# A state-space branch: decays in two half tiles of another pool, two chunks prepared ahead of the state, each chunk's norm at once

## The chip, the cores and the metric

The kernel runs on one core of one Trainium2 chip. The metric is device time in microseconds (us) of that core, from a run of the whole program. TensorE does the matrix products, VectorE, ScalarE and GpSimd (DVE, ACT and POOL in the rows) the elementwise work, and the queue of SyncE (SP) issues nearly all the DMAs.

## The reference

One layer of a recurrent decoder: 2048 prompt tokens and 32 sample tokens (8 sequences of 4) go through four branches in parallel (Mamba-2 SSD, S5, mLSTM, HGRN2), whose results are gated, added and projected out. The change is in the first branch. Its scan goes over chunks of 128 tokens, with 8 heads in 2 groups, and its result is gated and normalised per token:

```python
def step(h, inp):
    xc, ac, bc, cc = inp
    acum = jnp.cumsum(ac, axis=1)
    seg = acum[:, :, None] - acum[:, None, :]
    decay = jnp.exp(jnp.where(tri[None, :, :, None, None], seg, -jnp.inf))
    cb = jnp.einsum('btgn,bsgn->btsg', cc, bc)
    y = jnp.einsum('btsg,btsgr,bsgrp->btgrp', cb, decay, xc)
    y = y + jnp.einsum('btgn,bgrpn->btgrp', cc, h) * jnp.exp(acum)[..., None]
    to_end = jnp.exp(acum[:, -1:] - acum)
    h = h * jnp.exp(acum[:, -1])[..., None, None] + jnp.einsum('bsgn,bsgr,bsgrp->bgrpn', bc, to_end, xc)
    return h, y
...
h, ys = lax.scan(step, h0, (to_chunks(x, q), to_chunks(a, q), to_chunks(bm, q), to_chunks(cm, q)))
...
y = y + xs * p['ssd_D'].astype(F32).reshape(SSD_GROUPS, SSD_RPG, 1)
y = y.reshape(bsz, L, BRANCH_W) * jax.nn.silu(z.astype(F32))
y = rmsnorm(y, p['ssd_norm_w'])
```

## The kernel before

The prompt is worked on in four blocks of 512 tokens; block 0 carries the sample's 32 tokens too. Every dense product is done in three passes, with the weights and the inputs split into a high and a low part (`whi`, `wlo`, `xhi`, `xlo`): ScalarE makes `whi` (L122), VectorE and GpSimd make the two halves of `wlo` (L125, L127). The dense products that appear below are the merge gates `pg` (L284 to L286), the mLSTM's `pt_so` (L173 to L175) and S5's gate `pj_s5gs` (L147 to L149).

Each branch is a Python generator that gives way after a part of its work. Two strings, ORDER0 for block 0 and ORDER for the others, say which generator goes on next: `S` is the state-space mix `ssd_mix`, `M` the merge gates, `w` S5's set-up (block 0 alone), `q0` to `q3` S5's quarters, `m0` to `m3` the mLSTM's heads. A scheduler then sets the order on each engine from this program; on its engine an instruction never passes the one ahead of it, and a DMA waits in SP's queue until the buffer it writes is free. Tiles come from pools with a fixed number of buffers: `tm` has 4 of 1280 columns, of which the gate `zs` holds 2 for a whole block; `cm` has 13 of 544 columns; the PSUM pool of the small products has 5.

The mix of a block begins with sums of the decays, which are written to DRAM as rows (`arow`). Then, chunk by chunk, `ssd_core` loads the chunk's rows to all partitions as one tile `D` of 128x1024 in `tm` (L532), adds the mask on GpSimd (L535), and takes eight exponentials on ScalarE (L537). TensorE makes C B (`pc`, L542) and the transposed x (`px`, L548). ScalarE copies `px` to `xs`; VectorE makes `xdt` (L553), then `xde`, which needs the last column of every head's `D` (L557), then multiplies `D` by `pc` (L560, two halves). `yi` (L564) is eight products of `D` with `xdt`. The state follows: `yo` from the state `ssd_h` (L625) and the chunk's own part `st` from `xde` (L626); VectorE updates `ssd_h` (L629, L630). `ssd_y` puts y together, gates it with `zs` on GpSimd (L577) and takes its squares on ScalarE (L578). After the last chunk the norm of all chunks is one chain of 13 short instructions on VectorE (L636, L637 and `rsqrt`, L97 to L102), ScalarE scales `zs` (L641), and TensorE transposes it (`ypt`, L647). The mLSTM's rows `mlr` and `mlq` come right behind.

## Time and profile before

| | |
|---|---|
| time of three runs | 3214.97 us median (3210.85 to 3215.8) |
| profiled execution, first to last instruction | 3211.8 us, mean granted TensorE clock 0.968 |
| TensorE busy | 3054.7 us, 95% of the span |
| VectorE, GpSimd, ScalarE busy | 58%, 38%, 33% |
| DMA | 107 GB/s on average |

The profiled execution is one execution of the program; no time of its own is recorded beside its span, and the span lies within the three runs. TensorE is busy for nearly all of it, so a stretch in which it waits, or runs at the lower of its two clocks, shows directly in the time. The granted clock is given as a share of full speed (1.00 is 2.4 GHz, 0.50 is 1.2 GHz).

### The profile page before, as it was taken

The numbers are of one execution on the slowest core, as the hardware profiler recorded it, in microseconds if no ns is written. First come the engines' busy times: TensorE is split into PE (matmuls) and PEld (weight loads), VectorE is DVE, ScalarE is ACT, GpSimd is POOL, SyncE is SP. The second block draws the span as 40 slices with busy tenths as digits, with TensorE's granted clock in tenths as the row PEclk, the third lists the DMA queues.
The fourth block names the chain that finished last, engine by engine and source line by source line (L and its number), as shares of the span: only waits on it lengthen the run. The fifth ranks groups of instructions, "written<-read, shape, count | busy, mean of one in ns | idle before, by whom it ended". The sixth has DMA issues, their size and how long they took to land. (4 is left out here: it accounts for less than half of the span.)

```text
span 3211.8 us, 48779 instructions
## 1 busy us (share of the span) xinstructions
PE 3054.7 (95%) x18559; PEld 2652.6 (83%) x18559; DVE 1860.6 (58%) x3808; ACT 1067.7 (33%) x2200; POOL 1235.1 (38%) x1147
## 2 busy tenths in 40 slices
...
GB/s 163 96 96 189 125 90 96 88 65 95 120 99 199 151 50 92 117 84 87 79 111 179 144 86 86 117 87 79 79 105 156 156 129 71 92 80 74 100 93 86
DMA packets 204958, 344.68 MB, mean 107 GB/s; under 512 B 87908, under 2 KB 124676, under 8 KB 204724
## 3 DMA queue, kind: packets, MB, share of 16 engines
...
## 5 line engine op out<-in xcount | busy, mean ns | idle before, releaser
L127 POOL TENSOR_TENSOR wlo<-wraw,whi 128x384 fp32r<-128x384 f32 (+1 forms) x412 | 615.4, 1494 | 1196.7 <-ACT whi L122 1141.0
L125 DVE TENSOR_TENSOR wlo<-wraw,whi 128x640 fp32r<-128x640 f32 (+2 forms) x416 | 430.6, 1036 | 649.7 <-ACT whi L122 624.7
L122 ACT CAST whi<-wraw 128x1024 fp32r<-128x1024 f32 (+1 forms) x416 | 435.9, 1048 | 860.3 <-issue 319.3
L286 PE MATMUL pg<-xhi,wlo 128*128 128x512 f32 (+1 forms) x1280 | 463.1, 362 | 0.0
L284 PE MATMUL pg<-xhi,whi 128*128 128x512 f32 (+1 forms) x1280 | 461.9, 361 | 0.1
L285 PE MATMUL pg<-xlo,whi 128*128 128x512 f32 (+1 forms) x1280 | 458.9, 359 | 0.0
L286 PEld LDWEIGHTS pg<-xhi,wlo 128*128 128x128 f32 x1280 | 245.8, 192 | 35.9 <-issue 4.0
L285 PEld LDWEIGHTS pg<-xlo,whi 128*128 128x128 f32 x1280 | 245.7, 192 | 32.2 <-issue 0.9
L284 PEld LDWEIGHTS pg<-xhi,whi 128*128 128x128 f32 x1280 | 245.8, 192 | 31.2 <-issue 0.8
L326 PE MATMUL pb<-yh,whi 128*128 128x512 f32 (+1 forms) x640 | 227.2, 355 | 0.8 <-DVE acc L330 0.8
L328 PE MATMUL pb<-yh,wlo 128*128 128x512 f32 (+1 forms) x640 | 225.9, 353 | 0.0
L327 PE MATMUL pb<-yl,whi 128*128 128x512 f32 (+1 forms) x640 | 225.5, 352 | 0.0
L333 POOL TENSOR_TENSOR acc<-acc,gth 128x512 f32<-128x512 f32 (+1 forms) x120 | 138.4, 1154 | 192.3 <-DVE gth L332 169.3
L173 PE MATMUL po<-whi,mhi 128*128 128x256 f32 (+1 forms) x544 | 155.6, 286 | 8.1 <-ACT po L369 8.1
L174 PE MATMUL po<-wlo,mhi 128*128 128x256 f32 (+1 forms) x544 | 154.8, 284 | 0.0
L175 PE MATMUL po<-whi,mlo 128*128 128x256 f32 (+1 forms) x544 | 154.6, 284 | 0.0
L326 PEld LDWEIGHTS pb<-yh,whi 128*128 128x128 f32 x640 | 120.4, 188 | 18.2 <-issue 1.3
L327 PEld LDWEIGHTS pb<-yl,whi 128*128 128x128 f32 x640 | 120.4, 188 | 16.9 <-issue 0.6
L328 PEld LDWEIGHTS pb<-yh,wlo 128*128 128x128 f32 x640 | 120.3, 188 | 16.1
L332 DVE SCALAR_TENSOR_TENSOR gth<-gth,pb 128x512 f32<-128x512 f32 (+1 forms) x120 | 70.1, 584 | 94.3 <-PE pb L328 90.9
L877 POOL TENSOR_TENSOR hk<-hk,hC 128x256 f32<-128x256 f32 (+1 forms) x96 | 72.9, 759 | 110.9 <-PE hpa L854 53.1
L173 PEld LDWEIGHTS po<-whi,mhi 128*128 128x128 f32 (+1 forms) x544 | 102.0, 188 | 9.3 <-ACT po L369 8.8
...
## 6 DMA issues: line engine op xcount, KB each, us to landing
...
```

Of the source, the lines that this page charges most:

```text
L122: nc.scalar.copy(hi, raw)
L125: nc.vector.tensor_tensor(lo[:, :d], raw[:, :d], hi[:, :d].bitcast(F), op=OP.subtract)
L127: nc.gpsimd.tensor_tensor(lo[:, d:], raw[:, d:], hi[:, d:].bitcast(F), op=OP.subtract)
L173: nc.tensor.matmul(ps, xh, hi[:, k % 4], start=(k == 0), stop=False)
L174: nc.tensor.matmul(ps, xh, lo[:, k % 4], start=False, stop=False)
L175: nc.tensor.matmul(ps, xl, hi[:, k % 4], start=False, stop=(k == KT - 1))
L284: nc.tensor.matmul(pg, gh[:, k], self.xhi[k][:, o:o + n], start=(k == 0), stop=False)
L285: nc.tensor.matmul(pg, gh[:, k], self.xlo[k][:, o:o + n], start=False, stop=False)
L286: nc.tensor.matmul(pg, gl[:, k], self.xhi[k][:, o:o + n], start=False, stop=(k == KT - 1))
L326: nc.tensor.matmul(pb, bh[:, k], yh[k][:, o:o + n], start=(k == 0), stop=False)
L327: nc.tensor.matmul(pb, bh[:, k], yl[k][:, o:o + n], start=False, stop=False)
L328: nc.tensor.matmul(pb, bl[:, k], yh[k][:, o:o + n], start=False, stop=(k == 3))
```

## The change

- **D.** A chunk's decays are two tiles of 128x512 (`D_0`, `D_1`: a group of four heads each) in pool `cm`, each with its own DMA, its own mask on GpSimd and its own four exponentials.
- **xdt and xde.** Both are products with `px` straight from PSUM on VectorE. The factor of `xde` is a new small tile `dte` = exp(total - sum) * dt/8, made once in a block. ScalarE's copy `xs` serves the skip term alone. `xdt` and `xde` take turns in two role tiles each.
- **Order of the chunks.** `ssd_core` prepares a chunk; the new `ssd_chunk` does `yi`, `yo`, `st`, y and the state. They go 0, 1, then state 0, 2, state 1, 3, state 2, state 3, and the generator gives way after each.
- **Norm.** `ssd_y` ends with the chunk's own norm (13 short instructions for one column) and scaling.
- **Order strings.** In ORDER0 the S5 set-up `w` and the merge gates `M` stand elsewhere among the parts of `S`; in ORDER `S*2 M S*7` stands for `S M S*4`.

The rest of the file differs only in comments.

```diff
     def ssd_core(self, nb, c, m):
         nc = self.nc
         samp = m == NS
         o = c * P
         neg = self.negs if samp else self.neg
         nm = f"{nb}_{c}"
-        D = self.tm.tile([P, 1280], F, tag="tm", name=f"D{nm}", bufs=TMB)[:m, :8 * m]
-        self.dq.dma_start(D, self.arow[c // 4][8 * (c % 4):8 * (c % 4) + 8]
-                          .rearrange("h t -> (h t)").partition_broadcast(m))
-        D = D.rearrange("p (h t) -> p h t", h=8)
-        nc.gpsimd.tensor_tensor(D, D, neg.unsqueeze(1).to_broadcast([m, 8, m]), op=OP.add)
-        for h in range(8):
-            nc.scalar.activation(D[:, h], D[:, h], AF.Exp, bias=self.nac[:m, c, h:h + 1])
+        D = [self.cm.tile([P, TX], F, tag="cm", name=f"D{nm}_{g}", bufs=CMB)[:m, :4 * m] for g in range(2)]
+        for g in range(2):
+            r = 8 * (c % 4) + 4 * g
+            self.dq.dma_start(D[g], self.arow[c // 4][r:r + 4].rearrange("h t -> (h t)").partition_broadcast(m))
+            D[g] = D[g].rearrange("p (h t) -> p h t", h=4)
+            nc.gpsimd.tensor_tensor(D[g], D[g], neg.unsqueeze(1).to_broadcast([m, 4, m]), op=OP.add)
+            for h in range(4):
+                nc.scalar.activation(D[g][:, h], D[g][:, h], AF.Exp, bias=self.nac[:m, c, 4 * g + h:4 * g + h + 1])
         pc = self.psum(None, f"pc{nm}").rearrange("p (r t) -> p r t", r=4)[:m]
         BT, CT = self.xbc[4][:, o:o + m], [t[:, o:o + m] for t in self.CTm]
         for g in range(2):
@@ -547,22 +548,41 @@
         for j in range(4):
             nc.tensor.transpose(px[:, j * P:(j + 1) * P], self.xbc[j][:, o:o + m], self.ident)
         hv = lambda t: t.rearrange("p (h d) -> p h d", h=8)
+        mul = lambda e, out, v: e.tensor_tensor(hv(out), hv(px), v.unsqueeze(2).to_broadcast([m, 8, 64]), op=OP.mult)
+        xdt = self.role("be"[c % 2], f"xdt{nm}")[:m, :512]
+        mul(nc.vector, xdt, self.dtq[:m, c])
+        for g in range(2):
+            nc.vector.tensor_tensor(D[g], D[g], pc[:, g:g + 1, :m].to_broadcast([m, 4, m]), op=OP.mult)
+        xde = self.role("cf"[c % 2], f"xde{nm}")[:m, :512]
+        mul(nc.vector, xde, self.dte[:m, c])
         xs = self.role("a", f"xs{nm}")[:m, :512]
         nc.scalar.copy(xs, px)
-        xdt = self.role("b", f"xdt{nm}")[:m, :512]
-        nc.vector.tensor_tensor(hv(xdt), hv(xs), self.dtq[:m, c].unsqueeze(2).to_broadcast([m, 8, 64]), op=OP.mult)
         nc.gpsimd.tensor_tensor(hv(xs), hv(xs), self.Dh[:m].unsqueeze(2).to_broadcast([m, 8, 64]), op=OP.mult)
-        xde = self.role("c", f"xde{nm}")[:m, :512]
-        te = self.te_s if samp else D[:, :, 127]
-        nc.vector.tensor_tensor(hv(xde), hv(xdt), te.unsqueeze(2).to_broadcast([m, 8, 64]), op=OP.mult)
-        for g in range(2):
-            Dg = D[:, 4 * g:4 * g + 4]
-            nc.vector.tensor_tensor(Dg, Dg, pc[:, g:g + 1, :m].to_broadcast([m, 4, m]), op=OP.mult)
-        yi = self.psum(None, f"yi{nm}")[:m]
+        return D, xdt, xs, xde, Bt, CT
+    def ssd_intra(self, nb, c, m, D, xdt):
+        nc = self.nc
+        yi = self.psum(None, f"yi{nb}_{c}")[:m]
         for h in range(8):
             hs = slice(h * 64, (h + 1) * 64)
-            nc.tensor.matmul(yi[:, hs], D[:, h], xdt[:, hs], start=True, stop=True)
-        return yi, xs, xde, Bt, CT
+            nc.tensor.matmul(yi[:, hs], D[h // 4][:, h % 4], xdt[:, hs], start=True, stop=True)
+        return yi
+    def ssd_chunk(self, nb, c, dec, D, xdt, xs, xde, Bt, CT):
+        nc = self.nc
+        yo = self.psum(None, f"yo{nb}_{c}")
+        st = self.psum(None, f"st{nb}_{c}")
+        yi = self.ssd_intra(nb, c, P, D, xdt)
+        for g in range(2):
+            gs = slice(g * 64, (g + 1) * 64)
+            cs = slice(g * 256, (g + 1) * 256)
+            nc.tensor.matmul(yo[:, cs], CT[g], self.ssd_h, start=True, stop=True)
+            nc.tensor.matmul(st[gs, 0:256], Bt[:, gs], xde[:, cs], start=True, stop=True)
+        self.ssd_y(nb, c, P, yi, yo, xs)
+        hv = self.ssd_h.rearrange("p (r d) -> p r d", r=4)
+        nc.vector.tensor_tensor(hv, hv, dec[:, c].unsqueeze(2).to_broadcast([P, 4, 64]), op=OP.mult)
+        nc.vector.tensor_tensor(self.ssd_h, self.ssd_h, st[:, 0:256], op=OP.add)
...
             nc.scalar.activation(xs[:, qs], self.zs[q][:m, c], AF.Square, accum_out=self.yss[:m, q, c:c + 1])
 
+        v = self.sp.tile([P, 5], F, tag="yv", name=f"yv{nm}", bufs=2)
+        nc.vector.tensor_tensor(v[:m, 0:1], self.yss[:m, 0, c:c + 1], self.yss[:m, 1, c:c + 1], op=OP.add)
+        nc.vector.tensor_scalar(v[:m, 0:1], v[:m, 0:1], 1.0 / 512, 4 * EPS, op0=OP.mult, op1=OP.add)
+        rs = self.rsqrt(v[:, 0:1], "yr", m)
+        for q in range(2):
+            nc.scalar.mul(self.zs[q][:m, c], self.zs[q][:m, c], rs)
...
+        self.dte = self.sp.tile([P, 5, 8], F, tag="dte", name=f"dte{nb}", bufs=1)
+        nc.vector.tensor_tensor(fl(self.dte[:, 0:4]), fl(self.nac[:, 0:4]), pe[:, 32:64], op=OP.add)
+        nc.scalar.activation(fl(self.dte[:, 0:4]), fl(self.dte[:, 0:4]), AF.Exp)
+        nc.vector.tensor_tensor(self.dte[:, 0:4], self.dte[:, 0:4], self.dtq[:, 0:4], op=OP.mult)
...
         self.yss = self.sp.tile([P, 2, 5], F, tag="yss", name=f"yss{nb}", bufs=1)
-        if nb == 0:
-            nc.vector.memset(self.yss, 1.0)
         yield
-        for c in range(4):
-            yi, xs, xde, Bt, CT = self.ssd_core(nb, c, P)
-            yo = self.psum(None, f"yo{nb}_{c}")
-            st = self.psum(None, f"st{nb}_{c}")
-            for g in range(2):
-                gs = slice(g * 64, (g + 1) * 64)
-                cs = slice(g * 256, (g + 1) * 256)
-                nc.tensor.matmul(yo[:, cs], CT[g], self.ssd_h, start=True, stop=True)
-                nc.tensor.matmul(st[gs, 0:256], Bt[:, gs], xde[:, cs], start=True, stop=True)
-            self.ssd_y(nb, c, P, yi, yo, xs)
-            hv = self.ssd_h.rearrange("p (r d) -> p r d", r=4)
-            nc.vector.tensor_tensor(hv, hv, dec[:, c].unsqueeze(2).to_broadcast([P, 4, 64]), op=OP.mult)
-            nc.vector.tensor_tensor(self.ssd_h, self.ssd_h, st[:, 0:256], op=OP.add)
+        core = {}
+        for c in (0, 1, -1, 2, -2, 3, -3, -4):
+            if c >= 0:
+                core[c] = self.ssd_core(nb, c, P)
+            else:
+                self.ssd_chunk(nb, -1 - c, dec, *core.pop(-1 - c))
             yield
         if nb == 0:
             self.ssd_sample(nb)
-        v = self.sp.tile([P, 5], F, tag="yv", name=f"yv{nb}", bufs=1)
-        nc.vector.tensor_tensor(v[:, :ncc], self.yss[:, 0, :ncc], self.yss[:, 1, :ncc], op=OP.add)
-        nc.vector.tensor_scalar(v[:, :ncc], v[:, :ncc], 1.0 / 512, 4 * EPS, op0=OP.mult, op1=OP.add)
-        rs = self.rsqrt(v[:, :ncc], "yr")
-        for (c, o, m) in self.chunks(nb):
-            for q in range(2):
-                nc.scalar.mul(self.zs[q][:m, c], self.zs[q][:m, c], rs[:m, c:c + 1])
...
-        self.te_s = self.sp.tile([NS, 8], F, tag="te_s", name="te_s", bufs=1)
-        nc.scalar.activation(self.te_s, pe[:NS, 8:16], AF.Exp)
+        nc.scalar.activation(self.dte[:NS, 4], pe[:NS, 8:16], AF.Exp)
+        nc.vector.tensor_tensor(self.dte[:NS, 4], self.dte[:NS, 4], self.dtq[:NS, 4], op=OP.mult)
...
-        yi, xs, xde, Bt, CT = self.ssd_core(nb, 4, NS)
+        D, xdt, xs, xde, Bt, CT = self.ssd_core(nb, 4, NS)
+        yi = self.ssd_intra(nb, 4, NS, D, xdt)
...
-ORDER0 = ("z*2 i x*3 z w u x*3 u*2 S u S*3 w S*2 w*7 q2*2 q0 M q0*2 M*2 q1 M*5 q1 g0*8 q1 q2 q3 o q3*2 o*6 r "
+ORDER0 = ('z*2 i x*3 z w u x*3 u*2 w S u S*4 M S M S w S*5 M w*6 q2*2 q0 M q0*2 q1 M*4 q1 g0*8 q1 q2 q3 o q3*2 o*6 r
-ORDER = ("u x u z q0*2 x u q0 z q1*2 M z u x*3 q2*2 x q1 M*2 q3*3 M S M*2 q2 S M S*4 o r M m0 o m0 m1 m0*2 o "
+ORDER = ('u x u z q0*2 x u q0 z q1*2 M z u x*3 q2*2 x q1 M*2 q3*3 M S M*2 q2 S*2 M S*7 o r M m0 o m0 m1 m0*2 o
```

On TensorE, block 1, behind the state of chunk 0: before, the products `pc_1` and `px_1` that prepare chunk 1 come only here.

```order
L625 MATMUL yo_0_11894<-ssd_h,CT_0_11471 128x256
L626 MATMUL st_0_11895<-xde_0_11881,Bt_0_11869 64x256
L625 MATMUL yo_0_11894<-ssd_h,CT_1_11472 128x256
L626 MATMUL st_0_11895<-xde_0_11881,Bt_0_11869 64x256
L542 MATMUL pc_1_11955<-CT_0_11471,cv_xbc_1_11427 128x128
L542 MATMUL pc_1_11955<-CT_1_11472,cv_xbc_1_11427 128x128
L543 MATMUL pc_1_11955<-cst,cv_xbc_1_11427 128x128
L548 MATMUL px_1_11961<-cst,cv_xbc_1_10728 128x128
L548 MATMUL px_1_11961<-cst,cv_xbc_1_10971 128x128
L548 MATMUL px_1_11961<-cst,cv_xbc_1_11339 128x128
L548 MATMUL px_1_11961<-cst,cv_xbc_1_11383 128x128
```

After the change `pc_1` (and, 14 rows of S5 later, `px_1`) stands ahead of the first `yi`:

```order
L549 MATMUL px_0_11960<-cst,cv_xbc_1_11465 128x128
L543 MATMUL pc_1_11988<-CT_0_11553,cv_xbc_1_11509 128x128
L543 MATMUL pc_1_11988<-CT_1_11554,cv_xbc_1_11509 128x128
L544 MATMUL pc_1_11988<-cst,cv_xbc_1_11509 128x128
L284 MATMUL pg_0_6_0_12016<-xhi_0_10324,whi_12011 128x512
L285 MATMUL pg_0_6_0_12016<-xlo_0_10325,whi_12011 128x512
L286 MATMUL pg_0_6_0_12016<-xhi_0_10324,wlo_12013 128x512
L284 MATMUL pg_0_6_0_12016<-xhi_1_10331,whi_12011 128x512
```

and behind the state of chunk 0 stand only five products of S5's gate and the preparation of chunk 2, then `yi_1`:

```order
L543 MATMUL pc_2_12099<-CT_1_11554,cv_xbc_1_11509 128x128
L544 MATMUL pc_2_12099<-cst,cv_xbc_1_11509 128x128
L147 MATMUL pj_s5gs_1_0_12332<-xhi_0_10324,whi_12327 128x512
L148 MATMUL pj_s5gs_1_0_12332<-xlo_0_10325,whi_12327 128x512
L149 MATMUL pj_s5gs_1_0_12332<-xhi_0_10324,wlo_12329 128x512
L147 MATMUL pj_s5gs_1_0_12332<-xhi_1_10331,whi_12327 128x512
L148 MATMUL pj_s5gs_1_0_12332<-xlo_1_10332,whi_12327 128x512
L549 MATMUL px_2_12105<-cst,cv_xbc_1_10810 128x128
L549 MATMUL px_2_12105<-cst,cv_xbc_1_11053 128x128
L549 MATMUL px_2_12105<-cst,cv_xbc_1_11421 128x128
L549 MATMUL px_2_12105<-cst,cv_xbc_1_11465 128x128
L568 MATMUL yi_1_12121<-xdt_1_11999,D_1_0_11974 128x64 x4
```

So chunk 1's preparation moved ahead of chunk 0's state. Before, 20 rows of `pg` stood between `px_1` and `yi_1`; behind `yo_3`, after the change, stand 22 rows of `pg` with the transposes `ypt` and `mlr` among them, until the last `ypt` of chunk 3.

On SP's queue, block 1, with the semaphores that each DMA waits for (PE, DVE, Pool and Activation are engines, DMAHW other transfers), before:

```order
L1619 DMA s5c_2_11820<-dLC_1004 128x1024 [waits DMAHW5_49,PE_49]
L120 DMA wraw_12419<-in_win_dram 128x1024 [waits DMAHW3_49,DVE_49,Pool_49]
L532 DMA D_0_11854<-arow_11737 128x1024 [waits DMAHW4_49,DMAHW7_49,DMAHW0_49,PE_49]
L532 DMA D_1_11944<-arow_11737 128x1024 [waits DMAHW2_49,PE_49]
L1637 DMA s5gd_2_10655<-s5g_2_11822 128x8x64 [waits DMAHW6_49,DVE_49]
L1653 DMA s5gr_0_12172<-s5gd_0_10653 128x512
L1653 DMA s5gr_1_12413<-s5gd_1_10654 128x512 [waits Activation_49]
L120 DMA wraw_12459<-in_win_dram 128x1024 [waits DMAHW1_49,DVE_49,Pool_49]
L532 DMA D_2_12000<-arow_11737 128x1024 [waits DMAHW4_49,DVE_49,PE_49]
L120 DMA wraw_12506<-in_win_dram 128x1024 [waits DMAHW3_49,DVE_49,Pool_49]
L532 DMA D_3_12056<-arow_11737 128x1024 [waits DMAHW5_49,DVE_49,PE_49]
```

and after:

```order
L1637 DMA s5c_2_11906<-dLC_1004 128x1024 [waits DMAHW2_49,PE_49]
L534 DMA D_0_0_11940<-arow_11819 128x512 [waits DMAHW5_49,DMAHW0_49]
L534 DMA D_0_1_11941<-arow_11819 128x512 [waits DMAHW1_49]
L534 DMA D_1_0_11974<-arow_11819 128x512
L534 DMA D_1_1_11975<-arow_11819 128x512 [waits DMAHW3_49]
L534 DMA D_2_0_12085<-arow_11819 128x512 [waits DMAHW4_49]
L534 DMA D_2_1_12086<-arow_11819 128x512
L1671 DMA s5gr_0_12318<-s5gd_0_10735 128x512 [waits DMAHW6_49]
L1671 DMA s5gr_1_12559<-s5gd_1_10736 128x512 [waits DMAHW7_49,DVE_49]
L1655 DMA s5gd_2_10737<-s5g_2_11908 128x8x64 [waits DMAHW0_49,DVE_49]
L120 DMA wraw_12565<-in_win_dram 128x1024 [waits DMAHW1_49,Pool_49]
L534 DMA D_3_0_12162<-arow_11819 128x512 [waits DMAHW2_49,PE_49]
```

The loads of chunks 0 to 2 now stand in one piece behind `s5c_2` and wait for no engine; those of chunk 3 wait for TensorE, with a weight load ahead of them and another behind.

On VectorE, block 1, after the change: the short instructions of a chunk's norm (`yv_0`, `yr_t`, `yr_y`, 128x1) stand between the products that prepare chunk 3 and those of y and the state (`y`, `ssd_h`).

```order
L585 TENSOR_TENSOR ssd_h<-ssd_h,st_1_12120 128x256
L101 SCALAR_TENSOR_TENSOR yr_t<-yr_t,yv_0_12065 128x1
L551 TENSOR_TENSOR xdt_3_12187<-px_3_12182,dtq_11813 128x512
L102 SCALAR_TENSOR_TENSOR yr_y<-yr_t,yr_y 128x1
L555 TENSOR_TENSOR D_3_0_12162<-D_3_0_12162,pc_3_12176 128x512
L100 TENSOR_TENSOR yr_t<-yr_y 128x1
L555 TENSOR_TENSOR D_3_1_12163<-D_3_1_12163,pc_3_12176 128x512
L101 SCALAR_TENSOR_TENSOR yr_t<-yr_t,yv_0_12065 128x1
L601 TENSOR_TENSOR yv_1_12142<-yss_11835 128x1
L551 TENSOR_TENSOR xde_3_12191<-px_3_12182,dte_11828 128x512
L102 SCALAR_TENSOR_TENSOR yr_y<-yr_t,yr_y 128x1
L602 TENSOR_SCALAR yv_1_12142<-yv_1_12142 128x1
```

Before, the norm's instructions stood in one row behind all four chunks.

## Rows read from the trace of the kernel before

**Rows 1.** The page, busy time of each engine.
```profile
PE 3054.7 (95%) x18559; PEld 2652.6 (83%) x18559; DVE 1860.6 (58%) x3808; ACT 1067.7 (33%) x2200; POOL 1235.1 (38%) x1147
```

**Rows 2.** Windows of blocks 1 and 0: length, busy, TensorE clock, DMA share, GB/s.
```profile
1107.00:1191.00 84.00, 72.24 (x370) 57.74 (x370) 43.08 (x60) 32.86 (x87) 37.71 (x29) 0.84 0.24 79
...
117.00:266.00 149.00, 116.53 (x701) 98.44 (x700) 106.73 (x177) 57.16 (x182) 88.83 (x92) 0.80 0.40 104
```

**Rows 3.** TensorE's waits in block 1, 1107 to 1206: total, times, longest.
```profile
PE yi L564 <- ACT D L537: 6.0, 2, 3.5
PE yi L564 <- DVE D L560: 3.0, 1, 3.0
PE mlq L1042 <- ACT mlQ L1032: 2.1, 1, 2.1
PE ypt L647 <- ACT zs L641: 2.0, 1, 2.0
```

**Rows 4.** TensorE's waits in block 0, 117 to 266.
```profile
PE yi L564 <- ACT acc L287: 9.3, 1, 9.3
PE yi L564 <- issue: 6.7, 2, 3.8
PE ypt L647 <- ACT zs L641: 4.5, 1, 4.5
PE sts L713 <- DVE y L572: 3.8, 1, 3.8
```

**Rows 5.** Windows at either clock, columns as in rows 2.
```profile
217.00:223.80 6.80, 5.96 (x26) 5.78 (x26) 0.48 (x3) 4.79 (x11) 0.00 (x0) 0.50 0.66 97
...
1142.00:1152.20 10.20, 10.20 (x35) 7.65 (x35) 2.28 (x5) 1.76 (x6) 1.89 (x3) 0.50 0.30 103
...
1173.10:1177.30 4.20, 4.20 (x25) 2.98 (x25) 0.98 (x2) 0.66 (x2) 0.00 (x0) 1.00 0.00 0
...
1141.80:1149.40 7.60, 7.57 (x25) 5.14 (x25) 1.43 (x3) 1.24 (x5) 0.23 (x1) 0.51 0.41 138
```

**Rows 6.** Timelines around the first yi of block 1: start, length, [idle before].
```profile
1113.35 0.80 SPq L532 DMA_DIRECT2D D<-arow  x2
...
1119.74 2.46 ACT L537 ACTIVATE D<-D,nac 128x128 f32<-128x128 f32 x8 [1.27 <-POOL D L535]
...
1122.29 1.86 DVE L557 TENSOR_TENSOR xde<-xdt,D 128x512 f32<-128x512 f32 x1 [1.89 <-ACT D L537]
...
1125.13 2.15 PE L564 MATMUL yi<-xdt,D 128*128 128x64 f32 x9 [2.48 <-ACT D L537]
```

**Rows 7.** Timelines of GpSimd and VectorE ahead of chunk 1's yi.
```profile
1134.96 2.85 POOL L535 TENSOR_TENSOR D<-D,neg 128x1024 f32<-128x1024 f32 x1
...
1135.47 3.26 DVE L1665 TENSOR_TENSOR s5gs<-s5gs,s5gr 128x512 f32<-128x512 f32 x1
...
1138.65 1.22 DVE L557 TENSOR_TENSOR xde<-xdt,D 128x512 f32<-128x512 f32 x1
...
1141.05 1.27 DVE L560 TENSOR_TENSOR D<-D,pc 128x512 f32<-128x512 f32 x2
```

**Rows 8.** Timelines of VectorE and GpSimd at block 1's norm.
```profile
1184.03 1.01 POOL L127 TENSOR_TENSOR wlo<-wraw,whi 128x384 fp32r<-128x384 f32 x1 [1.09 <-ACT whi L122]
...
1182.00 0.97 DVE L636 TENSOR_TENSOR yv<-yss 128x4 f32<-128x4 f32 x1
...
1184.21 0.86 DVE L100 TENSOR_TENSOR yr_t<-yr_y 128x4 f32<-128x4 f32 x1
...
1185.88 0.16 DVE L102 SCALAR_TENSOR_TENSOR yr_y<-yr_t,yr_y 128x4 f32<-128x4 f32 x1
```

**Rows 9.** Timeline of VectorE, first and last instruction of block 0's norm.
```profile
207.63 0.20 DVE L636 TENSOR_TENSOR yv<-yss 128x5 f32<-128x5 f32 x1 [1.02 <-ACT xs L578]
...
217.09 0.15 DVE L102 SCALAR_TENSOR_TENSOR yr_y<-yr_t,yr_y 128x5 f32<-128x5 f32 x1
```

**Rows 10.** A product on VectorE that reads PSUM, block 1: ns min/median/max.
```profile
L572 DVE TENSOR_TENSOR y<-yo,ea x4: 690/692/692, 1131.9 to 1176.8; 128x512 f32<-128x512 f32 x4
```

More of the change, by code (lines that the diff above doesn't have):

```diff
@@ L633, in ssd_mix @@
             self.ssd_sample(nb)
-        v = self.sp.tile([P, 5], F, tag="yv", name=f"yv{nb}", bufs=1)
-        nc.vector.tensor_tensor(v[:, :ncc], self.yss[:, 0, :ncc], self.yss[:, 1, :ncc], op=OP.add)
-        nc.vector.tensor_scalar(v[:, :ncc], v[:, :ncc], 1.0 / 512, 4 * EPS, op0=OP.mult, op1=OP.add)
-        rs = self.rsqrt(v[:, :ncc], "yr")
-        for (c, o, m) in self.chunks(nb):
-            for q in range(2):
-                nc.scalar.mul(self.zs[q][:m, c], self.zs[q][:m, c], rs[:m, c:c + 1])
+            yield
         for j in range(4):
```

7 lines of the change are left out of this document (2 added, 5 removed).

## The prediction

> **What bounds the kernel now.** I read the page first: TensorE is busy for 95% of the span [rows 1], so a gain has to come from the 5% in which it waits, or from stretches in which its clock is low. The windows of the stages with the state-space chunks show both: the 84 us of block 1 have 72.2 us of TensorE work at a mean granted clock of 0.84, the 149 us of block 0 have 116.5 at 0.80 [rows 2]. Third come the waits in those windows. In block 1 TensorE waits 6.0 + 3.0 us for `yi`, 2.0 for `ypt` and 2.1 for `mlq` [rows 3]; blocks 2 and 3 repeat these rows to within 0.6 us, which makes 39 us for three blocks. Block 0 has 9.3 + 6.7 us at `yi`, 4.5 at `ypt` and 3.8 at `sts`, 24 in all [rows 4].
>
> Behind most of these waits the clock is 0.50, its lower level of 1.2 GHz: 6.8 us behind block 0's `ypt`, 10.2 us behind the wait for chunk 1 in block 1 [rows 5]. There are five such stretches in block 0 (47.7 us) and eleven in blocks 1 to 3 (85 us, three of them behind `mlq`). What one costs is read from two runs of the same 25 chunk products: 7.6 us at the lower level, 4.2 behind chunk 3's wait of only 0.8 us, where the clock stayed at 1.00 [rows 5]. That is 45% of the slow time: 38 us in blocks 1 to 3, 21 in block 0.
>
> **Why `yi` waits.** For chunk 0 it is the decay tile. Its DMA is issued at 1113.35, when a `tm` buffer comes free; the exponentials run from 1119.74, `xde` from 1122.29 because it needs their last column, and `yi` starts at 1125.13 [rows 6]. For chunk 1 it is VectorE. `px_1` comes only behind the state of chunk 0, and then S5's `s5gs`, `xde`, a weight part and the product `D` follow one another until 1142.3, the `s5gs` for 3.26 us because GpSimd's mask runs from 1134.96 to 1137.81 [rows 7].
>
> **The change part by part, blocks 1 to 3.**
> *Half tiles in the other pool.* On SP's queue the six loads of chunks 0 to 2 stand behind `s5c_2` and wait for no engine. Chunk 0's load no longer waits until 1113.35 for a buffer; the masks and exponentials of two halves are the same work as one tile's. More instructions on SP (two issues of 0.4 us for one, [rows 6]) cost nothing while the weight loads behind them are early; if that cover is gone they cost 4 x 0.4 = 1.6 us a block.
> *xdt and xde from PSUM.* The nearest row is `y<-yo`, a product of the same size that reads PSUM: 0.69 us, four times within 2 ns [rows 10]. `xde` took 1.86 and 1.22 [rows 6, 7]. I take 0.69 for both products, which frees some 6 us of VectorE in a block; at worst they cost what they cost now, and nothing is freed. The new `dte` is three short VectorE instructions in a block, under 1 us, long before it is needed.
> *Two chunks ahead.* `px_k`, `xdt` and `D*pc` are done a whole chunk before `yi_k`; 4.2 us of TensorE's chunk work then cover some 2.7 us of VectorE (two products of 0.69, two that take 1.27 together, [rows 7]). So all 9 us of `yi` waits go, and their slow stretches.
> *Norm per chunk.* This is the term that gives something back. Before, 13 short instructions took from 1182.00 to 1186.04, so 0.31 us each: most take 0.16, but `yr_t` took 0.86, ending with GpSimd's weight part (1184.03 + 1.01), and `yv` 0.97 [rows 8]. Now there are 52 in a block, on an engine that does not let the next product pass. Behind the state of chunk 2 the norms of chunks 2 and 3 are both still to do: 26 x 0.31 = 8.1 us, with y and the state (four products of 0.4 to 0.7, some 2.2) and two `s5gs` (0.7 and up to 3.3, [rows 7]) some 14 us. TensorE's cover behind `yo_3` is 22 merge products of 512 columns, at 2.4 GHz 0.21 us each, and the small transposes, about 7 us together. So `ypt` of chunk 3 waits about 7 us where it waited 2.0. Such a wait drops the clock once: 3 us more by the slow stretch of 6.8 us [rows 5]. I add 2 for small waits in between. This is 12 us a block. Its lower bound is 4, if a short instruction takes 0.16; its upper 21, if it takes 0.52, as in block 0: 9.6 us for 13 with 2.8 us of others among them [rows 9].
> *mlq.* The 96 `pt_so` products now stand between `mlr` and `mlq`, so its 2.1 us and the slow stretch go.
>
> Together: 39 of waits and 38 of clock, 77 removed, less 3 x 12 given back, leaves 41.
>
> **Block 0.** 24 us of waits and 21 of clock, 45, are the upper bound. But VectorE is busy for 106.7 of 149 us there [rows 2], and S5's set-up, which now stands behind the chunks, is VectorE work. The 13 short instructions (6.8 us) become 65, 20 to 34 us at 0.31 to 0.52, and ten products save some 7. VectorE then has 113 to 127 us of work. It is now 72% busy, since it too waits for the chunks; with their waits gone I let it reach 90%, so the stage takes 125 to 141 us, 8 to 24 less. I take 15. At today's 72% it would be longer than now; I keep -10 as the lower bound.
>
> **Sum.** 41 + 15 = 56 us. The profiled execution's span of 3211.8 lies 3 us below the median, inside the runs; the difference is taken from the median: 3215 - 56 = 3159.
>
> **Two rules weighed.** On VectorE and GpSimd, [rows 8] show a VectorE instruction of 0.16 us that ends 0.03 us after GpSimd's, and [rows 7] one that ends behind the mask. The Trainium skill, "SBUF — State Buffer", section "SBUF: two separate sides", says that an instruction of VectorE with two SBUF inputs and one of GpSimd exclude each other for the whole instruction. These rows agree. By the row's mean of 0.31 us the sum stands; by the rule at its worst, every short instruction meeting a GpSimd one, the norm would cost what the slower rival below says. On the clock, [rows 5] show 1.00 behind a wait of 0.8 us and 0.50 behind waits of 3.5 and 4.5 us [rows 3, 4]. The Trainium skill's "TensorE: Matmul & The Clock Gate", section "A second HAM failure mode: psum-queue depth-cycling", says that short idle moments between groups of matmuls, as PSUM buffers go round, can keep the clock moving between its levels. Chunk 3's run in block 1 does not show that; by the rule the outcome is the clock rival below.
>
> **The rivals.**
> *Nothing given back.* The short instructions fall between GpSimd's, put-back 4 us a block, and block 0 gains 30: 65 + 30 = 95, 3120 us. For it: without `yv` and the one of 0.86, the other 11 of block 1 share 2.2 us [rows 8]. Against it: GpSimd's 37.7 us of work in the stage now fall into some 62 us instead of 84.
> *The waits move.* Short instructions at 0.52, put-back 21 us, and block 0 gains nothing because S5's set-up is late: 14 us, 3201. The same time would come out if the decays in fact waited for `cm` buffers; for chunks 0 to 2 the queue speaks against that.
> *The clock stays low.* Waits go, slow stretches do not: 39 less 3 x 9, and 8 in block 0, 20 in all: 3195.
> *Slower.* VectorE becomes the bound of the chunk stages because GpSimd shuts its short instructions out. In block 1 it has 43.1 us of work [rows 2]; without the old norm (4.0) and 6 for the products, 33, and 52 short ones. At GpSimd's mean of 37.7/29 = 1.3 us each this is 101 us, 17 more than the 84 of the stage; three blocks 50, and block 0 (106.7 - 6.8 - 7 + 65 x 1.3 = 177) 28: 3215 + 78, about 3293. It decides from about 1.0 us an instruction (33 + 52 = 85). No mean near that is in the rows; single ones of 0.86 and 0.97 are.
>
> **How the numbers follow.** Forecast 3159, own range 3140 to 3181 (put-back 9 to 16, block 0 5 to 25): 0.52. Nothing given back 0.20, waits move 0.14, clock stays low 0.06, slower 0.06; the last 0.02 for a change that does nothing. A measurement of this kernel can tell about 0.2%, 6.4 us. The moved waits and the low clock reach across that bound to both sides, by a third of their chance. Faster 0.86, same 0.05, slower 0.09. For 8 in 10 the range goes from 3108 (beyond the second case) to 3195 (the low clock, short of the moved waits).
>
> **What would show it.** Right: no wait of over 1 us at `yi` in blocks 1 to 3; a granted clock of 0.95 or so in the chunk stages; `xdt` and `xde` at 0.69; a wait of about 7 us at chunk 3's `ypt`, and none at `mlq`. Wrong: 52 short instructions with a mean far from 0.31, `yi` waiting for `D` or a pool, or S5's set-up in block 0 ending no earlier than now. Were the clock to drop without a wait ahead of it, the reading of the slow stretches would be wrong.

## The result

The changed kernel takes 3170.4 us (median of four runs, 3166.0 to 3175.7) against 3212.9 before (3207.9 to 3215.8): a ratio of 0.9874 with a 95% interval of 0.9858 to 0.9890. The forecast was 3159, with a range of 3108 to 3195. The profiled execution's span is 3166.6 us, 45 us shorter than that of before.

Window of the kernel after, of block 1's chunk stage (columns as in rows 2):

```profile
1104.60:1170.80 66.20, 59.29 (x364) 46.68 (x362) 48.70 (x117) 35.92 (x94) 38.00 (x36) 1.00 0.37 110
```

Block 1's stage, which answers to the first of [rows 2], takes 66 us instead of 84, with a granted clock of 1.00 instead of 0.84. Both windows hold the products of all four chunks, but not the same dense products between them, so this comparison is a rough one. Block 0 comes further below, with windows of equal work. TensorE's waits in block 1 after the change, which answer to [rows 3]:

```profile
PE mlq L1060 <- ACT mlQ L1050: 2.9, 1, 2.9
PE s5y L1645 <- DMA s5c<-dLC: 2.7, 1, 2.7
PE pea L635 <- DVE dte L632: 1.8, 1, 1.8
PE px L549 <- DVE yr_t L97: 1.7, 1, 1.7
PE yo L580 <- ACT zs L605: 0.9, 1, 0.9
PE ypt L664 <- ACT zs L605: 0.8, 1, 0.8
```

No wait for `yi` of over 0.4 us is left there. In their place stand four short waits, at `pea`, `px`, `yo` and `ypt`; `mlq`'s is longer than before, and `s5y`'s lies ahead of the chunks. In block 0 waits for `yi` remain (these answer to [rows 4]):

```profile
PE s5pt L1490 <- DVE s5Xr L1338: 10.3, 3, 4.3
PE yi L568 <- DVE D L555: 3.7, 3, 2.8
PE pea L635 <- DVE dte L632: 3.4, 1, 3.4
PE yi L568 <- ACT xs L559: 3.2, 1, 3.2
```

To see where the time went I compare, in the two traces, when each block's first output product `po` starts: 905.2, 1663.0, 2411.2 and 3156.2 us before, 911.6, 1650.6, 2378.3 and 3111.0 after. So block 0 is 6.4 us late, and blocks 1 to 3 are 18.8, 20.5 and 12.3 us shorter, 51.6 together. TensorE over these three blocks, before and then after, each row the sum of three windows:

```profile
sum 2251.00, PE 2168.59 PEld 1825.33 DVE 1281.64 ACT 747.30 POOL 874.68; mean PE 722.86 PEld 608.44 DVE 427.21 ACT 249.10 POOL 291.56
...
sum 2199.40, PE 2133.96 PEld 1797.47 DVE 1264.75 ACT 748.92 POOL 875.44; mean PE 711.32 PEld 599.16 DVE 421.58 ACT 249.64 POOL 291.81
```

Its idle time fell from 82.4 to 65.4 us, by 17.0. The other 34.6 us are the same products in less busy time, at a higher granted clock (0.99 in the three blocks instead of 0.97). So two thirds of the gain came through the clock.

The start of `po` is the measure for every experiment too; it comes from one profiled execution each, whose span can lie some 7 us from the median of its runs, so differences of a few us in it mean little.

### The profile page after: what moved, and what is told of

Its sections match the earlier page's. It is cut to its first block, busy times and chain, and to the rows that moved or that the text cites. A ratio compares the mean times of both kernels' runs of the same rounds, so it can differ in the third digit from the quotient of the medians.

```text
span 3166.6 us, 49000 instructions
## 1 busy us (share of the span) xinstructions
PE 3029.8 (96%) x18559; PEld 2634.1 (83%) x18559; DVE 1845.6 (58%) x3985; ACT 1070.9 (34%) x2204; POOL 1232.1 (39%) x1164
## 5 line engine op out<-in xcount | busy, mean ns | idle before, releaser
L127 POOL TENSOR_TENSOR wlo<-wraw,whi 128x384 fp32r<-128x384 f32 (+1 forms) x412 | 625.4, 1519 | 1209.9 <-ACT whi L122 1163.5
L125 DVE TENSOR_TENSOR wlo<-wraw,whi 128x640 fp32r<-128x640 f32 (+2 forms) x416 | 411.0, 988 | 694.7 <-ACT whi L122 664.9
```

The source lines that it names most:

```text
L125: nc.vector.tensor_tensor(lo[:, :d], raw[:, :d], hi[:, :d].bitcast(F), op=OP.subtract)
L127: nc.gpsimd.tensor_tensor(lo[:, d:], raw[:, d:], hi[:, d:].bitcast(F), op=OP.subtract)
```

## The experiments

The ratio is to runs of the kernel before that were taken beside each kernel (medians of 3211.5 to 3214.7 us). The last two columns are differences to before in the traces.

| kernel | median, us | ratio to before (95%) | block 0, us | blocks 1 to 3, us |
|---|---|---|---|---|
| after | 3170.4 | 0.9874 (0.9858 to 0.9890) | +6.4 | -51.6 |
| e1 chunks one after another | 3176.3 | 0.9888 (0.9852 to 0.9924) | +14.9 | -44.5 |
| e2 products as before | 3176.1 | 0.9898 (0.9863 to 0.9933) | +8.2 | -47.0 |
| e7 both of these undone | 3214.1 | 0.9996 (0.9985 to 1.0007) | +33.8 | -27.5 |
| e6 old pool, whole tile | 3170.1 | 0.9861 (0.9838 to 0.9885) | +1.7 | -50.3 |
| e5 half tiles alone | 3209.5 | 0.9984 (0.9972 to 0.9996) | +6.7 | -10.9 |
| e9 products from PSUM alone | 3171.2 | 0.9879 (0.9863 to 0.9895) | -0.1 | -36.8 |
| e10 two chunks ahead alone | 3195.9 | 0.9950 (0.9935 to 0.9965) | +6.8 | -20.0 |
| e4 block 0's old string | 3168.6 | 0.9871 (0.9842 to 0.9899) | +2.6 | -46.8 |
| e3 norm at the block's end | 3155.5 | 0.9831 (0.9797 to 0.9865) | +0.6 | -49.8 |
| e8 e3 and dte later | 3154.0 | 0.9811 (0.9792 to 0.9831) | -1.2 | -57.0 |
| e11 e8 and block 0's old string | 3165.4 | 0.9859 (0.9844 to 0.9875) | +8.4 | -58.0 |
| e12 norm a chunk later, dte later | 3158.8 | 0.9834 (0.9818 to 0.9851) | +4.2 | -59.0 |

My theory at the start was the prediction's: preparing two chunks ahead takes the waits away (A). The rivals: the early loads do (B, later H), or the products from PSUM (C).

**e1, the order of the chunks undone.**

```diff
-        for c in (0, 1, -1, 2, -2, 3, -3, -4):
+        for c in (0, -1, 1, -2, 2, -3, 3, -4):
```

> The changed kernel with its chunks in the order of before: chunk c is prepared, then its state is done, then the next one (half tiles, products from PSUM, norm per chunk stay). Theory A, the gain of blocks 1 to 3 comes from preparing two chunks ahead: px of a chunk stands behind the state of the one before again, the wait for xdt and D*pc (about 2.7 us) shows at yi, with slow clock behind it, some 10 to 14 us a block: 3200 to 3215. Theory B, early loads and products from PSUM are enough: no wait over 1 us at yi in blocks 1 to 3, at most 3180.

Measured: 3176, and in block 1 no wait over 0.7 us at `yi`. Theory A as I had put it fell; B held.

**e2, the products undone.**

```diff
-        mul(nc.vector, xdt, self.dtq[:m, c])
+        nc.vector.tensor_tensor(hv(xdt), hv(xs), self.dtq[:m, c].unsqueeze(2).to_broadcast([m, 8, 64]), op=OP.mult)
...
-        mul(nc.vector, xde, self.dte[:m, c])
+            for g in range(2):
+                nc.vector.tensor_tensor(h4(xde), h4(xdt), D[g][:, :, 127].unsqueeze(2).to_broadcast([m, 4, 64]), op=OP.mult)
```

> The changed kernel with xdt from ScalarE's copy and xde from xdt and the last column of D, as before, for the prompt's chunks. Theory A (order): D is ready a chunk ahead, so xde's wait for the exponentials is hidden; VectorE has 4 to 6 us more of work in a block, px's buffers come free later, and the time rises by 1 to 5 us a block: 3173 to 3185. Theory C (the products from PSUM carry the gain): yi or st waits again, 3195 or more.

Measured: 3176, inside A's range, so C in its strong form fell as well. Taken one at a time, neither part seemed to carry the gain.

**e5, the half tiles alone, put into the kernel before.** The edit is the change's own block for `D`, with `xde` made in two halves from the last columns.

> The kernel before with one part of the change alone: D as two half tiles in the other pool (xde in two halves from their last columns). Undoing the order of the chunks and undoing the products from PSUM cost 6 us each, so neither carries the gain. Theory H, the early loads carry it: yi no longer waits for more than 1 us in blocks 1 to 3, 3180 or less. Theory J, the parts stand in for one another, and VectorE's line behind px (s5gs, xde, weight part, D*pc) keeps the waits for chunks 1 and 2: only the wait for chunk 0 goes (2.5 us and its slow stretch of 6.8 us), some 5 to 6 us a block: 3192 to 3202.

Measured: 3209.5, so the early loads (H) don't carry it either. The waits of block 1:

```profile
PE yi L568 <- DVE D L564: 4.1, 2, 2.9
...
PE ypt L651 <- ACT zs L645: 3.2, 1, 3.2
...
PE mlq L1046 <- ACT mlQ L1036: 3.1, 1, 3.1
```

`yi` still waits for VectorE's `D`, as J had it, but the time lies above J's range: in blocks 1 to 3 the traces differ by 10.9 us, and 6.7 of them are lost in block 0.

**e6, the old pool and the whole tile in the changed kernel.**

```diff
-        D = [self.cm.tile([P, TX], F, tag="cm", name=f"D{nm}_{g}", bufs=CMB)[:m, :4 * m] for g in range(2)]
+        D = self.tm.tile([P, 1280], F, tag="tm", name=f"D{nm}", bufs=TMB)[:m, :8 * m]
...
+        D = [D[:, 0:4], D[:, 4:8]]
```

> The changed kernel with D as one 128x1024 tile in the old pool of four buffers. Theory H (early loads): the load of chunk 0 waits for S5's buffers until about 1113 again, those of chunks 2 and 3 for yi of 0 and 1; yi waits 2 us and more two or three times a block, 3190 or more. Theory J (the parts stand in for one another): preparing ahead and the products from PSUM leave VectorE ready, only yi of chunk 0 waits, some 5 us a block: 3180 to 3190.

Measured: 3170.1, no difference to the change that these runs can tell, so both theories missed. A wait at `yi` of chunk 0 comes back, and `pc` waits 2.3 us; in their place those at `px` (1.7) and `mlq` (2.9) are gone or small (0.6 at `mlq`):

```profile
PE yi L568 <- DVE D L555: 1.8, 1, 1.8
```

Beside the other two parts the half tiles are worth nothing that this can tell; J's 10 to 20 us for this part did not come.

**e7, order and products both undone.**

> The changed kernel with both undone that cost 6 us each: chunks in the order of before, and xdt and xde from ScalarE's copy and D. Half tiles and the norm per chunk stay. Theory H: early loads are enough, the two costs add: about 3182. Theory J: each stood in for the other, with both gone the waits of yi for chunks 1 and 2 come back, 3190 or more.

Measured: 3214.1. One undone costs 6 us, hardly more than these runs can tell; both cost 44: each stands in for the other, as J had it. First two rows: block 1; last: block 0.

```profile
PE yi L574 <- DVE D L565: 2.6, 2, 1.9
...
PE yi L574 <- ACT xs L604: 2.2, 1, 2.2
...
PE yi L574 <- DVE D L565: 12.0, 3, 7.6
```

The waits for `D` are back in both. But by the two traces, which lie 52 us apart where the medians lie 44, only 24 us of that are in blocks 1 to 3, and 27 in block 0. With both parts gone blocks 1 to 3 are still 27.5 us shorter than before, and the half tiles alone (e5) gave 10.9. The other 17 must come from what e7 keeps and e5 lacks: the norm per chunk, the finer parts of the generator and the new string of blocks 1 to 3 (`S*2 M S*7`). In block 1 e7 has no wait at `mlq` (e5 3.1 us), 5.4 at `yi` (e5 7.0) and 1.8 at `ypt` (e5 3.2). That string stays as changed in every run but e5, so what it is worth alone was not tested.

**e9, the products from PSUM alone.** From the changed kernel, nearly all else is undone: chunks one after another, `D` in the old pool, the norm at the end (e3), block 0's old string (e4); `dte` stands as in e8. What stays, here and in e10, is the string of blocks 1 to 3.

> One part of the change alone: xdt and xde from PSUM with the small factor dte (made behind the transposes of the sums); D is one tile of the old pool, chunks one after another, norm at the end, block 0's string as before. By blocks, undoing this part or the order alone cost 5 to 7 us in blocks 1 to 3, undoing both 24. Theory J (either stands in for the other): this part alone brings most of the gain of blocks 1 to 3, 40 us or more, and block 0 no loss: 3165 to 3178. Theory L (each carries half, and the rest of the change the rest): 3185 to 3195.

Measured: 3171.2, as fast as the whole change and inside J's range, with 37 us in blocks 1 to 3 (J had 40 or more) and none lost in block 0. VectorE's timeline behind `px_1` in block 1 (start, length) shows how:

```profile
1127.98 0.69 DVE L551 TENSOR_TENSOR xdt<-px,dtq 128x512 f32<-128x512 f32 x1 [0.91 <-PE px L549]
1128.59 1.27 DVE L555 TENSOR_TENSOR D<-D,pc 128x512 f32<-128x512 f32 x2
1129.78 0.68 DVE L551 TENSOR_TENSOR xde<-px,dte 128x512 f32<-128x512 f32 x1
```

`D` is done 1.9 us after `xdt` begins. In [rows 7] the same piece of line had `s5gs`, `xde` and a weight part in it, and took 6.9 us from the start of `s5gs` to 1142.3. `xde`, which no longer needs the exponentials, stands behind `D`, and so does `s5gs`, at 1131.46; whether the string had a part in that order isn't shown. Chunk 0's `yi` keeps a wait, as its exponentials still come some 13 us behind `pc_0`:

```profile
1119.34 1.10 PE L568 MATMUL yi<-xdt,D 128*128 128x64 f32 x8 [1.72 <-DVE D L555]
```

**e10, two chunks ahead alone.** As e9, with the products of before and the new order of chunks.

> The other part alone: two chunks prepared ahead of the state; xdt from ScalarE's copy, xde from D (the prompt's chunks), D one tile of the old pool, norm at the end, block 0's string as before. Theory J: most of the gain of blocks 1 to 3 again, 3165 to 3178. Theory L: 3185 to 3195. Between the two parts: where the order alone leaves VectorE's long xde and xdt, the wait is at px or pc, whose PSUM tiles come free late.

Measured: 3195.9, just above theory L's range. In block 1:

```profile
1125.40 4.79 ACT L537 ACTIVATE D<-D,nac 128x128 f32<-128x128 f32 x16 [4.13 <-POOL D L535]
...
1126.77 1.22 DVE L563 TENSOR_TENSOR xde<-xdt,D 128x256 f32<-128x256 f32 x1 [5.04 <-ACT D L537]
```

With the whole tile in the old pool the exponentials are late here (1125.4), `xde` still needs them, and VectorE sits idle for 5.0 us ahead of it. `yi` of block 1 waits 4.5 us in all, where it waited 9.8 before. e2, which has the half tiles and their early loads (and the norm per chunk), gained 47 us in blocks 1 to 3 with the same products. So the order needs either the early loads or the products; the products bring 37 of the change's 52 us in blocks 1 to 3 with neither.

**e4, block 0's old string.**

```diff
-ORDER0 = ('z*2 i x*3 z w u x*3 u*2 w S u S*4 M S M S w S*5 M w*6 q2*2 q0 M q0*2 q1 M*4 q1 g0*8 q1 q2
+ORDER0 = ('z*2 i x*3 z w u x*3 u*2 S u S*6 w S*4 w*7 q2*2 q0 M q0*2 M*2 q1 M*5 q1 g0*8 q1 q2
```

> The changed kernel with the order string of block 0 as before (its parts of S mapped: setup, u, six parts, w, the last four; merge gates and S5's set-up where they were). Blocks 1 to 3 are unchanged. Theory E, block 0 is late because the new string puts S5's four quarters of set-up in one piece behind the chunks, so that TensorE waits for VectorE there: block 0 ends 5 to 15 us earlier, 3155 to 3165. Theory F, VectorE's work (65 short instructions among it) is the bound of block 0 in either order: within 4 us of 3170. Theory G, the new string is what fills the waits of block 0's chunks: later by 5 us or more, over 3175.

Measured: 3168.6. Theory F's bound is met; whether VectorE is the reason, this doesn't say (e11 will go against it).

**e3, the norm at the end of the block again** (the 13 short instructions of `ssd_y` go, the old lines behind the last chunk come back).

> The changed kernel with the norm of all chunks at the end of the block, as before. Theory A: 39 short instructions less in a block, so the waits of px (yv stands ahead of xde) and of mlq (its chain stands behind the norm on VectorE) shrink, but ypt waits for the norm again, 3 to 4 us; nearly even in blocks 1 to 3, block 0 some 5 us earlier: 3160 to 3172. Theory D (the norm per chunk is what removes the tail): ypt waits 5 us and more with a slow clock behind it, 3180 or more.

Measured: 3155.5, 15 us faster than the change and below A's range (the two intervals of the ratio overlap a little; that of e8 below lies clear of the change's). In block 1:

```profile
PE ypt L666 <- ACT zs L660: 3.6, 1, 3.6
```

`ypt` waits 3.6 us instead of 0.8, but the waits at `px`, `yo` and `mlq` are gone or small (0.5 at `mlq`). In the one profiled execution block 0 is 6 us earlier and blocks 1 to 3 are even; the medians differ by more than that, and I have no better split.

**e8, dte behind the transposes too.**

```diff
-        self.dte = self.sp.tile([P, 5, 8], F, tag="dte", name=f"dte{nb}", bufs=1)
-        nc.vector.tensor_tensor(fl(self.dte[:, 0:4]), fl(self.nac[:, 0:4]), pe[:, 32:64], op=OP.add)
...
+        self.dte = self.sp.tile([P, 5, 8], F, tag="dte", name=f"dte{nb}", bufs=1)
+        nc.vector.tensor_tensor(fl(self.dte[:, 0:4]), fl(self.nac[:, 0:4]), pe[:, 32:64], op=OP.add)
...
         self.yss = self.sp.tile([P, 2, 5], F, tag="yss", name=f"yss{nb}", bufs=1)
```

> The changed kernel with the norm at the end of the block (3155 measured) and, new, the small factor dte made behind the transposes that share its PSUM tile. Theory K: the sums' transposes (pea) waited 3.4 and three times 1.8 us for dte only because it reads the tile they write; now at most 0.6 each, as before the change, so 5 to 7 us less: 3148 to 3152. Rival: dte moves from one wait to another (xde, and with it the state, waits for it): no change, 3155.

Measured: 3154.0, the fastest version here, but above K's range. `pea` of block 1 waits 0.5 us instead of e3's 1.7 (in block 0 it still waits 3.4, now for `nac`):

```profile
PE pea L625 <- DVE nac L623: 0.5, 1, 0.5
```

The wait is shorter by 1.2 us in the trace; the 1.5 us between the medians of e3 and e8 are less than their spread can tell, so K's reading of the wait held and its 5 to 7 us did not show.

**e11, e8 with block 0's old string.**

> The best version so far (norm at the end of the block, dte behind the transposes, 3154) with block 0's string of before. In block 0 both strings came out even with the norm per chunk (2.6 against 6.4 us later than before in one execution each). Theory F (VectorE's S5 set-up is the bound of block 0 in either order): within 5 us of 3154. Theory E (the new string is late): 3140 to 3149.

Measured: 3165.4, so both F and E were wrong: with the norm at the end the new string is worth some 10 us in block 0. Waits of block 0 in e11:

```profile
PE ypt L666 <- ACT zs L660: 6.4, 1, 6.4
...
PE yo L580 <- DVE ssd_h L585: 4.8, 1, 4.8
...
PE s5y L1647 <- DMA s5H<-in_s5h_dram: 4.8, 1, 4.8
```

With the old string `yo` waits 4.8 us (0.3 in e8), `ypt` 6.4 (4.4) and S5's `s5y` 4.8 for its state. Set beside e9, e11 has the half tiles and the order of the chunks in addition, and nothing else: blocks 1 to 3 are 21 us shorter by the traces, block 0 is 8.5 longer, and the medians lie 5.8 apart.

**e12, the norm per chunk, written one chunk later** (a method `ssd_norm`, called for chunk c behind the state of chunk c+1; `dte` as in e8).

> The norm per chunk as changed, but written one chunk later in the program (and dte behind the transposes), so that its first instruction yv, which waits for ScalarE's squares, no longer stands ahead of the next chunk's xde on VectorE. Theory M (what the norm per chunk costs is its place in VectorE's line): px's waits of 0.4 to 1.7 us go, 3150 to 3158. Theory N (it is the 52 short instructions themselves, at the end of the block above all, with mlq's chain behind them): mlq waits 3 us or more, 3160 to 3168.

Measured: 3158.8, 0.8 us above M's upper end and short of N's range. The 52 short instructions are all there; `px` and `mlq` no longer wait, `mlr` waits 1.5 us, and `ypt` this:

```profile
PE ypt L671 <- ACT zs L608: 2.5, 1, 2.5
```

So most of what the norm per chunk costs is its place in the line: this and the norm at the end win back 12 and 15 us, in e12 with the small share of `dte`'s move.

## Why the prediction was right, point by point

**Right in size and direction, by two errors that partly cancel.** Forecast: 41 us from blocks 1 to 3 and 15 from block 0. The traces give 51.6 and -6.4. That the sum came within 12 us of the time is luck in part. Split as the forecast splits it, blocks 1 to 3 were to give 12 us of waits (39 less 3 x 9) and 29 of clock (38 less 3 x 3). Measured are 17.0 and 34.6, so the mechanism was right there too: two thirds of what the waits cost was slow clock.

**Waits and clock.** That the waits of `yi` and the slow stretches behind them would go was right: none over 0.4 us is left in block 1, and the clock of its stage is 1.00. The reading of [rows 5], slow stretches as a consequence of waits, held here as an order in time (no run changes the clock by itself): with the waits gone and the stage denser the clock stayed up, so the rival of a low clock fell in blocks 1 to 3. In block 0 it did not fall (below).

**Two chunks ahead.** "So all 9 us of `yi` waits go" was put under this part. That attribution was wrong. In e9, with the products from PSUM and without the order, only chunk 0's wait is left in each block (1.7, 1.7 and 2.7 us); in e10, with the order and without the products, 4.5, 5.2 and 4.3 us are left. What I had read in [rows 7], VectorE's line behind `px`, was the cause for chunk 1; the shortest remedy for it was the other edit. The share of the string of blocks 1 to 3 in both stays open.

**xdt and xde.** I took 0.69 us each from `y<-yo`. Measured over the program:

```profile
L551 DVE TENSOR_TENSOR xdt<-px,dtq x17: 672/687/692, 125.2 to 2598.2; 128x512 f32<-128x512 f32 x16, 32x512 f32<-32x512 f32 x1
...
L551 DVE TENSOR_TENSOR xde<-px,dte x17: 672/681/685, 125.8 to 2601.7; 128x512 f32<-128x512 f32 x16, 32x512 f32<-32x512 f32 x1
```

**Norm per chunk.** The put-back was mis-sized. Of the 12 us a block, 7 was a wait at `ypt`; it is 0.8. The 52 short instructions of block 1 take 12.7 us in the timeline, 0.24 each, where I took 0.31. The norms of chunks 2 and 3 are both still to do behind the state of chunk 2, as forecast: chunk 2's begins only at 1150.16, next to y of chunk 3. But from that state (1148.57) to the last short instruction VectorE needs 11.0 us, not 14, and TensorE has 10.3 us of work from `yo_3` (1148.72) to the last `ypt` (1160.27, less two waits of 1.3 us together), not 7. What the norm per chunk costs lies elsewhere. VectorE's timeline after, with the idle time ahead in brackets:

```profile
1128.40 0.68 DVE L592 TENSOR_TENSOR y<-yo,ea 128x512 f32<-128x512 f32 x1
...
1135.97 0.41 DVE L601 TENSOR_TENSOR yv<-yss 128x1 f32<-128x1 f32 x1 [3.83 <-ACT xs L598]
...
1136.96 0.68 DVE L592 TENSOR_TENSOR y<-yo,ea 128x512 f32<-128x512 f32 x1
...
1150.16 0.15 DVE L601 TENSOR_TENSOR yv<-yss 128x1 f32<-128x1 f32 x1
...
1150.70 0.69 DVE L592 TENSOR_TENSOR y<-yo,ea 128x512 f32<-128x512 f32 x1
...
1159.45 0.16 DVE L102 SCALAR_TENSOR_TENSOR yr_y<-yr_t,yr_y 128x1 f32<-128x1 f32 x1
1159.53 1.26 DVE L1024 TENSOR_TENSOR_SCAN mlm<-mllf,mcar,mli 4x512 f32<-4x512 f32 x1
```

The second row is `yv` of chunk 0, which waits 3.8 us for ScalarE's squares. Behind it on the line stand `xde` of chunk 2 and then `y<-yo` of chunk 1. That product ends at 1137.64, and TensorE's `px_3`, which waited 1.7 us, starts at 1137.69. In e12, where no `yv` stands ahead of it, `y<-yo` of chunk 1 waits only for GpSimd's `zs`, and `px_3` follows without a gap in TensorE's work. Its rows, VectorE's of chunks 0 and 1 and then TensorE's:

```profile
1126.15 0.68 DVE L592 TENSOR_TENSOR y<-yo,ea 128x512 f32<-128x512 f32 x1
...
1133.17 0.69 DVE L592 TENSOR_TENSOR y<-yo,ea 128x512 f32<-128x512 f32 x1 [2.50 <-POOL zs L597]
...
1134.13 0.60 PE L549 MATMUL px<-cst,cv_xbc 128*128 128x128 f32 x4
```

In e12 `y<-yo` of chunk 1 starts 7.0 us after that of chunk 0, in the kernel after 8.6 (1136.96 less 1128.40), and the difference of 1.6 us is about the wait at `px`. In e3 and e8 too `px_3` starts 0.2 to 0.5 us behind the end of this product, never ahead of it, so I take it that it goes into the PSUM buffer that `yo` of chunk 1 leaves; the listed releaser `yr_t` is only what started at that moment. The prediction named neither `yv`'s wait nor what stands behind it. The last row of VectorE's timeline after is the first instruction of `mlq`'s chain, behind the last short one. I had `mlq`'s wait gone; it is 2.9 us. In e3, e8 and e12, which move the short instructions, it is 0.5 or none. In e9 and e10, which have no short instructions there either but other edits undone, `mlq` waits 3.1, so the short ones are one way to be late for `mlq` and not the only one.

**dte.** That it comes "long before it is needed" was right and beside the point: its read of the sums holds back the transposes into the same PSUM tile. `pea` waits 1.8 us in block 1, where it waited 0.6 before; e8, where the read comes later, shows 0.5. The 3.4 us in block 0 have another cause.

**Block 0.** The step that failed is "with their waits gone I let it reach 90%", with the 15 us taken from it. Windows of equal TensorE work (721 and 722 products), from the first chunk product to the last one of S5's set-up and from there to S5's first gate product (`s5gl`), first before, then after; the last two rows are all of block 0, before and after:

```profile
116.70:269.70 153.00, 120.53 (x721) 102.40 (x720) 108.82 (x180) 58.87 (x190) 89.08 (x92) 0.79 0.41 108
269.70:360.80 91.10, 84.71 (x658) 83.07 (x658) 64.85 (x134) 25.03 (x55) 32.35 (x34) 0.95 0.63 182
...
123.30:269.30 146.00, 122.17 (x722) 103.99 (x720) 103.49 (x225) 60.02 (x190) 85.45 (x97) 0.79 0.41 117
269.30:367.00 97.70, 90.21 (x659) 88.25 (x657) 68.56 (x134) 24.94 (x55) 32.48 (x34) 0.89 0.60 165
...
0.00:905.20 905.20, 840.23 (x6273) 781.76 (x6274) 557.35 (x1401) 302.32 (x733) 340.76 (x389) 0.96 0.37 111
...
0.00:911.60 911.60, 850.11 (x6273) 791.15 (x6274) 557.44 (x1455) 303.89 (x734) 336.96 (x394) 0.95 0.37 110
```

The stage is 7.0 us shorter, not 8 to 24. VectorE has 103.5 us of work in it, not 113 to 127, and is busy for 71% of it, as before. TensorE's idle time there fell from 32.5 to 23.8 us, but the clock stayed at 0.79, so of the 21 us of clock none came.

The rest was lost where the forecast put nothing. Ahead of the stage it is 6.6 us. The forecast has S5's set-up "now" behind the chunks; seven of its parts (`w`) stood there before too, and the new string moves one of them ahead of the sums of the decays, where VectorE does it before `nac`. With the old string (e4) `nac` comes 2.3 us earlier, `pea` waits 0.5 us instead of 3.4, and the first chunk product starts at 118.2 instead of 123.3. VectorE's rows after, then two rows of e4:

```profile
114.45 0.23 DVE L1338 TENSOR_TENSOR s5pw<-s5pw,s5t 128x64 f32<-128x64 f32 x1
...
115.33 0.18 DVE L629 TENSOR_SCALAR nac<-pea 128x32 f32<-128x32 f32 x1
...
113.03 0.18 DVE L629 TENSOR_SCALAR nac<-pea 128x32 f32<-128x32 f32 x1
...
PE pea L635 <- DVE dte L632: 0.5, 1, 0.5
```

Behind the set-up another 6.6 us are lost, 5.5 of them as more busy time at a lower clock. The set-up itself waits 10.3 us at `s5pt`, 6.7 before, and its last product starts at 269.0 instead of 269.4: it ends no earlier, which was one of the forecast's own signs of being wrong. Over all of block 0 TensorE is idle for 3.5 us less and busy for 9.9 more with the same 6273 products. So what the waits gave, the clock took: in block 0 the rival of the low clock came true in kind. Why the clock fell there stays open. Neither string, nor the pool, nor the norm made block 0 more than 1.2 us shorter than before.

**Rivals.** The slower one, GpSimd shutting out every short instruction, fell: 0.24 us is far from its 1.0. Nothing given back (3120) fell with block 0. The moved waits (3201) fell by their time, though block 0 gained nothing, as they had it.
